# Hybrid decoder block in float32: turning the attention and retention tiles by VectorE and DRAM, and a new order on SyncE's queue

## The chip, the core and the metric

The kernel runs on one core of one Trainium2 chip. The metric is the device time of one execution in microseconds (us). PE is the matrix engine TensorE, DVE is VectorE, ACT is ScalarE, POOL is GpSimd, and SP is SyncE, which here only issues DMA transfers.

## What is computed

One decoder block over 256 tokens of width 2048, all in float32, cut here to its skeleton:

```
h = x
h = h + 0.5 * swiglu(rms_norm(h, ffn1_norm), ffn1_w_gate, ffn1_w_up, ffn1_w_down)      # width 5632
n = rms_norm(h, mix_norm)
rq, rk, rv, rg, sq, sk, sv = split(n @ w_in)          # 4 x 1024, 1024, 128, 128 columns
ret = retention(rope(rq), rope(rk), rv)               # 8 heads of 128, chunks of 128 tokens
ret = silu(rg) * group_norm(ret) * ret_gn_gain
swa = sliding_window_attention(rope(sq), rope(sk), sv, sinks)   # 16 heads of 64, 2 kv heads, window 128
h = h + concat(ret, swa) @ w_out
h = h + memory_cross_attention(rms_norm(h, xa_norm), rms_norm(mem, mem_norm), wq, wkv, wo)   # 4 heads of 512, 256 memory tokens
h = h + 0.5 * swiglu(rms_norm(h, ffn2_norm), ffn2_w_gate, ffn2_w_up, ffn2_w_down)
out = rms_norm(h, final_norm)
```

## The kernel before

**Three products for one.** Float32 precision is made from a format that PE multiplies quickly (float32r): every operand is held as a high part and a rest. A product is three matmuls (`three`, lines 456 to 458): high by high, rest by high, high by rest. Activations stand as `blk` tiles (128 x 4 blocks x 2 parts x 256 tokens).

**Steps.** The weights stream through the core once. SP loads 1 MB at a time into `wf` (128 x 2 x 1024, 3 buffers), which serves two steps. For each step ACT copies the piece into `wh` (line 70) and DVE makes `wl = wf - wh` (line 75), 4 buffers of each. A step is 12 matmuls of 512 columns into an `acc` tile, and the whole program is 772 steps: FFN1 up to step 264, then the mixer's projections (window keys, values and the first window queries to 276, the other window queries to 284, retention's queries and keys to 300, its values and gate to 316 for four heads, the same for the other four to 348), `w_out` to 380, the cross attention's keys to 412, values to 444, queries to 476, output projection to 508, FFN2 from there to the end. In `run_stream`, `prepare` issues loads and splits so that the split of a step stands three steps ahead of its use (`LOOKAHEAD = 3`).

**The order of everything else.** A clock counts steps. `later(delay, fn)` puts a task on a list, and `run_due` emits the due tasks between two steps. What a task emits for PE, ACT and DVE is pinned behind the last instruction emitted for that engine; the splits are not pinned and are placed by the scheduler. On SP and POOL the DMAs stand in the order in which the scheduler comes to them.

**Turning.** Results come with the tokens on the partitions and are wanted with the features there. `cross` does this for most tiles: DVE turns 32 x 32 blocks of a 128 x 512 tile (STREAM_TRANSPOSE, line 437), POOL's queue writes the tile to a DRAM `box` (line 439) and reads it back in four DMAs in another order (line 444), and the consumer runs `TURN = 6` steps after. Four kinds of tiles are turned on PE instead, against an identity matrix: the window attention's probabilities (`swa_group.second`, line 632), its queries, as high and rest parts (`turned` in `sq_done`, line 682), retention's output (`turn`, line 327) and the cross attention's probabilities (`attend.probs`, line 882).

**Norms.** `Norm.stat` squares (ACT) and adds (DVE) into `sums`; `Norm.finish` sums over partitions with matmuls against ones (line 397), two steps after the last block; `spread` turns the row of scales (line 413).

**Memory tokens.** While `w_out` runs, `mem_block` loads the 256 memory tokens in eight pieces into `t2k` tiles (line 805, on SP), from which nmem's blocks are made (line 349).

Of the kernel before, what the change touches and what calls it, by code (L numbers as in the profile page):

```python
# [17 lines left out]
P = 128  # L18
S = 256
# [10 lines left out]
LOOKAHEAD = 3  # L30
TAIL = 4
WARM = 9
FIRST = 16
TURN = 6
# [4 lines left out]
def decoder_block(ctx: ExitStack, tc: tile.TileContext, a: dict, out: bass.AP):  # L39
# [40 lines left out]
    identr = const.tile([P, P], F32R, tag="identr", name="identr")  # L80
# [8 lines left out]
    nc.vector.tensor_copy(identr, ident)  # L89
# [141 lines left out]
    def run_stream():  # L231
# [22 lines left out]

        def prepare(upto):
            while nxt[0] < min(upto, len(steps)):
                at = nxt[0]
                if at == len(loaded):
                    u, piece = steps[at][0], steps[at][3]
                    if u.pair:  # L260
                        loaded.extend(load_pair(u.w, piece))
                        continue
                    two = at + 1 < len(steps) and steps[at + 1][0] is u and steps[at + 1][3] == piece + 1
                    loaded.extend(load(u.w, piece, 1 + two))
# [16 lines left out]
        for at, (u, b, ks, _, first, last) in enumerate(steps):  # L281
# [4 lines left out]
            else:  # L286
# [3 lines left out]
                prepare(at + 1 + LOOKAHEAD)  # L290
            run_until(lambda: b in u.lhs)
# [30 lines left out]
    def turn(src):  # L322

        tp = [tmp_ps() for _ in range(2)]
        for kk in range(4):
            for t in range(2):
                nc.tensor.transpose(
                    tp[kk // 2][:, (kk % 2) * S + t * P : (kk % 2) * S + (t + 1) * P], src(t, kk), ident
                )
        return tp  # L330

# [19 lines left out]
    class Norm:  # L351
# [4 lines left out]
        def __init__(self, gcol, name, spread=True):  # L356
            self.gcol, self.spreads = gcol, spread
# [19 lines left out]
        def stat(self, src):  # L377
# [10 lines left out]
            if self.left == 0:  # L388
                later(2, self.finish)

        def finish(self):

            tp = tmp_ps()
            for t in range(2):
                for i in range(2):
                    at = i * S + t * P
                    nc.tensor.matmul(  # L397
                        tp[:, t : t + 1], self.sums[:, at : at + P], ones[:, :1], start=i == 0, stop=i == 1
                    )
# [7 lines left out]
        def spread(self):  # L407
# [6 lines left out]
            self.rows = work.tile([P, S], F32, tag="rows", name=nm("rows"), bufs=2)  # L414
# [14 lines left out]
    def cross(src, then, room=None, delay=TURN):  # L429
# [4 lines left out]
        out, boxes = [], []  # L434
        for i, v in enumerate(src):
            sq = t2k()
            nc.vector.transpose(sq.rearrange("p (g q j) -> p q g j", g=4, q=4), squares_of(v))  # L437
            box = dram.tile([P, 512], F32, tag="box", name=nm("box"))
            nc.gpsimd.dma_start(box, sq)  # L439
            boxes.append(box.rearrange("(i r) (g n) -> g r i n", i=4, g=4))  # L440
        for i, box in enumerate(boxes):
            dst = t2k() if room is None else room[i]
            for g in range(4):
                nc.gpsimd.dma_start(dst[32 * g : 32 * g + 32, :].rearrange("p (i n) -> p i n", i=4), box[g])  # L444
            out.append(dst.rearrange("p (i q j) -> p q i j", i=4, q=4))
# [70 lines left out]
    n1 = Norm(G_FFN1, "n1", spread=False)  # L516
    for b in range(4):
# [4 lines left out]
        later(4 * b + (b < 3), lambda b=b: n1.stat([hT[b]]))  # L522
# [9 lines left out]
    nmix = Norm(G_MIX, "nmix")  # L532
# [59 lines left out]
    def swa_group(g, t, heads, q, probs):  # L592
# [473 lines left out]
```

## Time and profile before

| | before |
|---|---|
| median of 3 runs | 2206.41 us (2206.3 to 2208.78) |
| profiled execution, its own time | 2206.03 us |
| its span in the profile | 2204.2 us |
| PE busy | 2182.6 us (99%) |
| DVE busy | 1291.2 us (59%) |
| ACT busy | 1027.3 us (47%) |
| POOL busy | 309.6 us (14%) |

PE is busy nearly all of the span. A stretch of the profile is read by asking how long PE stands idle in it, what it then waits for, and what the engine that it waits for had in front. The stages lie at these times: FFN1 to 729 us, the mixer's projections from there to 998, `w_out` to 1094, the cross attention to 1473, FFN2 behind it.

### The profile page before, as it was taken

Reading aid. Unit: us, or ns where it says so; the run is one execution under the profiler, and the core shown is the slowest. Engines: PE = TensorE matmul, PEld = TensorE weight load, DVE = VectorE, ACT = ScalarE, POOL = GpSimd, SP = SyncE. Lnnn points to the kernel's source line nnn. Section 1 sums busy time; section 2 is a strip of 40 time slices with the busy share of each in tenths; the row PEclk is TensorE's granted clock in tenths of the full one; section 3 lists DMA queues with packets and bytes.
Section 4 is the critical chain, followed back from the end, with each engine's and each line's share of the span. In section 5 each row is a group of like instructions: output and inputs, shape, how many; then the busy total and the mean of one; then the engine's idle time right before and its main releaser. Section 6 shows DMA issues by size and latency. Waiting matters only on the chain.

```text
span 2204.2 us, 25835 instructions
## 1 busy us (share of the span) xinstructions
PE 2182.6 (99%) x9868; PEld 1807.8 (82%) x9868; DVE 1291.2 (59%) x1535; ACT 1027.3 (47%) x1260; POOL 309.6 (14%) x557
## 2 busy tenths in 40 slices
PE   9999999999999999999999999999999999999998
PEld 7888888888888888888788888887888888888886
DVE  5555555555556779786655555565555544555554
ACT  6444444444445554544545554454544433444443
POOL 0200111011011110111231011123201000000100
PEclk9999999999999999999999999999999999999999
DMA  7766677666677555556776555577766655666663
GB/s 268 230 218 211 210 230 234 216 212 233 210 234 245 208 193 172 179 185 196 234 252 230 196 191 191 190 247 232 260 217 224 215 191 193 214 208 223 213 217 143
DMA packets 132731, 472.04 MB, mean 214 GB/s; under 512 B 15616, under 2 KB 16384, under 8 KB 132480
## 3 DMA queue, kind: packets, MB, share of 16 engines
q1 hardware_dynamic: 109856, 413.57, 54.8%
q0 software_dynamic: 22464, 56.66, 8.8%
q8 instruction: 77, 1.26, 0.2%
q14 instruction: 46, 0.38, 0.1%
q10 hardware_dynamic: 288, 0.18, 0.0%
HBM read 439.93 MB, written 30.41 MB: 213 GB/s over the span
## 4 chain that ended last, share of the span: by engine, by line
PE 88%; issue 5%; DMA 3%; DVE 2%; ACT 1%; POOL 1%; SPq 0%; ACTq 0%; POOLq 0%; DVEq 0%
PE acc L457 28%; PE acc L456 28%; PE acc L458 28%; DMA wf<-in_w_out 1%; DVE wl L75 1%; DMA t2k<-box 1%; DMA wf<-in_ffn_w_up 1%; ACT wh L70 1%; POOL t2k L444 1%; PE tmp L458 0%; PE tmp L457 0%; PE tmp L456 0%; PE tmp L397 0%; PE tmp L632 0%; PE tmp L606 0%
## 5 line engine op out<-in xcount | busy, mean ns | idle before, releaser
L75 DVE TENSOR_TENSOR wl<-wf,wh 128x1024 fp32r<-128x1024 f32 (+1 forms) x776 | 941.2, 1217 | 793.0 <-ACT wh L70 789.7
L70 ACT ACTIVATE wh<-wf 128x1024 fp32r<-128x1024 f32 (+1 forms) x776 | 815.8, 1055 | 977.0 <-PE acc L458 916.8
L456 PE MATMUL acc<-wh,blk 128*128 128x512 f32 (+1 forms) x3104 | 1209.7, 390 | 4.4 <-ACT wh L70 3.5
L457 PE MATMUL acc<-wl,blk 128*128 128x512 f32 (+1 forms) x3104 | 1207.2, 389 | 2.5 <-DVE wl L75 2.5
L458 PE MATMUL acc<-wh,blk 128*128 128x512 f32 (+1 forms) x3104 | 1206.4, 389 | 0.0
L456 PEld LDWEIGHTS acc<-wh,blk 128*128 128x128 f32 x3104 | 583.9, 188 | 125.5 <-ACT wh L70 4.9
L457 PEld LDWEIGHTS acc<-wl,blk 128*128 128x128 f32 x3104 | 583.9, 188 | 123.0 <-DVE wl L75 4.7
L458 PEld LDWEIGHTS acc<-wh,blk 128*128 128x128 f32 x3104 | 583.8, 188 | 120.2 <-DVE blk L349 0.2
L439 POOL DMA_DIRECT2D box<-t2k x108 | 60.8, 563 | 1516.1 <-DVE t2k L437 1483.2
L444 POOL DMA_DIRECT2D t2k<-box x432 | 236.0, 554 | 122.6 <-issue 47.0
L70 ACT ACTIVATE blk<-t2k 128x512 fp32r<-128x512 f32 (+2 forms) x74 | 45.1, 614 | 59.8 <-DMA t2k<-box 58.1
L437 DVE STREAM_TRANSPOSE t2k<-t2k 128x512 f32<-128x512 f32 x76 | 49.4, 687 | 19.0 <-ACT t2k L70 19.0
L75 DVE TENSOR_TENSOR blk<-t2k,blk 128x512 fp32r<-128x512 f32 (+1 forms) x66 | 43.7, 674 | 26.1 <-ACT blk L70 26.0
L493 ACT ACTIVATE t2k<-acc,n 128x512 f32<-128x512 f32 x44 | 27.8, 685 | 29.4 <-PE acc L458 29.4
L500 DVE SCALAR_TENSOR_TENSOR t2k<-acc,n,t2k 128x512 f32<-128x512 f32 x44 | 31.0, 746 | 7.7 <-PE acc L458 7.7
L70 ACT ACTIVATE blk<-h,gains 128x256 fp32r<-128x256 f32 x64 | 27.4, 496 | 8.7 <-DVE h L467 8.7
L70 ACT ACTIVATE blk<-tmp 128x512 fp32r<-128x512 f32 (+2 forms) x49 | 21.7, 450 | 20.2 <-DVE blk L75 14.4
L349 DVE SCALAR_TENSOR_TENSOR blk<-h,gains,blk 128x256 fp32r<-128x256 f32 x64 | 26.8, 478 | 0.0
L467 DVE TENSOR_TENSOR h<-h,t2k 128x512 f32<-128x512 f32 x32 | 21.1, 687 | 9.0 <-DMA t2k<-box 8.7
L386 DVE TENSOR_TENSOR t2k<-t2k,t2k 128x512 f32<-128x512 f32 x35 | 24.1, 687 | 1.9 <-ACT t2k L382 0.6
L75 DVE TENSOR_TENSOR blk<-tmp,blk 64x256 fp32r<-64x256 f32 (+2 forms) x41 | 19.2, 474 | 3.0 <-ACT blk L70 2.8
L382 ACT ACTIVATE t2k<-h 128x512 f32<-128x512 f32 x32 | 18.2, 616 | 2.6 <-DVE h L467 2.6
(125 smaller groups left out, 495.2 us busy)
## 6 DMA issues: line engine op xcount, KB each, us to landing
wf<-in_ffn_w_down SPq DMA_DIRECT2D x88, 1024.0 KB, 4.9
wf<-in_ffn_w_gate SPq DMA_DIRECT2D x87, 1024.0 KB, 5.1
wf<-in_ffn_w_up SPq DMA_DIRECT2D x87, 1024.0 KB, 5.6
box<-t2k POOLq DMA_DIRECT2D x108, 256.0 KB, 2.9
t2k<-box POOLq DMA_DIRECT2D x432, 64.0 KB, 4.9
wf<-in_w_in_rqk SPq DMA_DIRECT2D x16, 1024.0 KB, 5.0
wf<-in_w_in_rvg SPq DMA_DIRECT2D x16, 1024.0 KB, 5.0
wf<-in_w_out SPq DMA_DIRECT2D x16, 1024.0 KB, 5.3
```

Source lines behind the costliest of these rows:

```text
L70: return nc.scalar.activation(dst, src, AF.Copy, **kw)
L75: nc.vector.tensor_tensor(lo, src, hi, ALU.subtract)
L349: nc.vector.scalar_tensor_tensor(x[:, k, 1, :], v[:, k, :], g, x[:, k, 0, :], ALU.mult, ALU.subtract)
L386: nc.vector.tensor_tensor(self.sums, self.sums, y, ALU.add)
L437: nc.vector.transpose(sq.rearrange("p (g q j) -> p q g j", g=4, q=4), squares_of(v))
L439: nc.gpsimd.dma_start(box, sq)
L444: nc.gpsimd.dma_start(dst[32 * g : 32 * g + 32, :].rearrange("p (i n) -> p i n", i=4), box[g])
L456: nc.tensor.matmul(o, ah, bh, start=start, stop=False)
L457: nc.tensor.matmul(o, ah, bl, start=False, stop=False)
L458: nc.tensor.matmul(o, al, bh, start=False, stop=stop)
L493: nc.scalar.activation(gated[b][t], acc[:, t, :], AF.Silu, scale=norm.scale(t))
L500: nc.vector.scalar_tensor_tensor(s[t], acc[:, t, :], norm.scale(t), s[t], ALU.mult, ALU.mult)
```

## The change

1. **Queues.** `cross` becomes three tasks: DVE turns at once, `write` puts the box on SP's queue one step later, `read` puts the four reads there two steps later, and the consumer runs after `TURN = 5`. POOL issues no DMA any more; SP issues 1076 rather than 420.
2. **Loads written ahead.** `fetch` issues a load four steps (`AHEAD = 4`) before its split is prepared, so that loads stand 8 steps ahead of their use in the program.
3. **Turning.** Window probabilities, window queries, retention's output and the cross attention's probabilities go through `cross`; `turn` and `identr` are gone. Window queries are split into halves after the turning rather than before. STREAM_TRANSPOSE of tiles in SBUF goes from 76 to 100. PE loses 84 float32 transposes and 32 of the queries' kind.
4. **Norms.** `finish` first adds the two halves of `sums` on DVE and needs two matmuls rather than four; its delay is given for each norm (2, 3 or 4 steps). Only nmix spreads its scales.
5. **Smaller moves.** The memory tokens are loaded into `blk` tiles, four DMAs rather than eight; the blocks of `w_out` run 0, 2, 3, 1; nxa's blocks are made during the keys; retention's scores start a step later; `swa_values` runs four steps after the probabilities.
6. **Queries ahead of values.** The cross attention projects keys, queries, values, where it was keys, values, queries. `attend` makes scores and softmax when a query block is there, and `values` multiplies when the value block is there.

The core of the diff:

```diff
+AHEAD = 4
-TURN = 6
+TURN = 5
...
             prepare(at + 1 + LOOKAHEAD)
+            fetch(at + 1 + LOOKAHEAD + AHEAD)
...
         def finish(self):
+            x = self.sums
+            nc.vector.tensor_tensor(x[:, :S], x[:, :S], x[:, S:], ALU.add)
             tp = tmp_ps()
             for t in range(2):
-                for i in range(2):
...
+                nc.tensor.matmul(tp[:, t : t + 1], x[:, t * P : (t + 1) * P], ones[:, :1], start=True, stop=True)
...
+        sq = [t2k() for _ in src]
+        for x, v in zip(sq, src):
+            nc.vector.transpose(x.rearrange("p (g q j) -> p q g j", g=4, q=4), squares_of(v))
+        def write():
+            for x in sq:
+                boxes.append(dram.tile([P, 512], F32, tag="box", name=nm("box")))
+                nc.sync.dma_start(boxes[-1], x)
+        def read():
+            for box, dst in zip(boxes, room):
...
+                for g in range(4):
+                    nc.sync.dma_start(dst[32 * g : 32 * g + 32, :].rearrange("p (i n) -> p i n", i=4), far[g])
...
+        later(1, write)
+        later(2, read)
         later(delay, lambda: then(out))
...
-        def second():
-            tp = tmp_ps()
-            for n in range(4):
-                nc.tensor.transpose(tp[:, n * P : (n + 1) * P], s[:, n * P : (n + 1) * P], ident)
+        def second(out):
...
-        later(5, second)
+        cross([s], second, [s])
...
-            later(5, lambda: turned(0))
-            later(6, lambda: turned(1))
+            cross(rs, turned, rs)
...
-                tp = turn(lambda t, kk: ret[t][:, kk * P : (kk + 1) * P])
-                mixT[g] = split_turned(tp, G_GN + 4 * g)
-            later(3, turned)
...
+            cross(ret, turned)
...
-            nc.sync.dma_start(m[i], a["mem"][b * P : (b + 1) * P, 2 * i : 2 * i + 2, :])
+        m = st["mem"][:, 4 * (b % 2) : 4 * (b % 2) + 4, :]
+        nc.sync.dma_start(m, a["mem"][b * P : (b + 1) * P])
...
-    for i in range(4):
-        Unit(a["xa_wv"], i, 512, nmem.blocks, v_done(i), range(4))
...
     for i in range(4):
         Unit(a["xa_wq"], i, 512, nxa.blocks, put_done(nxa, queries, i, lambda i=i: attend(i)), range(4), pair=True)
+    for i in range(4):
+        Unit(a["xa_wv"], i, 512, nmem.blocks, v_done(i), range(4))
```

**How it stands on the engines: DVE at the window attention beside retention (step 326).** In the rows, `wl` names are splits, `tmp` and `m`, `den`, `es` belong to the softmax of one window group. Before:

```order
L75 TENSOR_TENSOR wl_1155_6832<-wf_1153_6829,wh_1154_6831 128x1024
L616 TENSOR_REDUCE m_1146_6806<-t2k_1143_6797 128x2
L75 TENSOR_TENSOR wl_1157_6848<-wf_1153_6829,wh_1156_6847 128x1024
L617 TENSOR_TENSOR m_1146_6806<-m_1146_6806,sinks_83 128x2
L618 TENSOR_SCALAR nmx_1147_6807<-m_1146_6806 128x2
L619 TENSOR_TENSOR es_1149_6809<-sinks_83,m_1146_6806 128x2
L75 TENSOR_TENSOR wl_1163_6885<-wf_1161_6882,wh_1162_6884 128x1024
L623 TENSOR_TENSOR den_1148_6808<-den_1148_6808,es_1149_6809 128x2
```

After, the end of a stretch of 19 rows (26 instructions) that begins with the masks of the group and has no weight split in it:

```order
L625 TENSOR_TENSOR den_1188_6991<-den_1188_6991,es_1189_6992 128x2
L626 RECIPROCAL den_1188_6991<-den_1188_6991 128x2
L627 TENSOR_TENSOR t2k_1183_6980<-t2k_1183_6980,den_1188_6991 128x512
L786 SCALAR_TENSOR_TENSOR blk_1178_6934<-t2k_1169_6873,gains_79,blk_1178_6934 128x128 x4
L76 TENSOR_TENSOR blk_901_5562<-tmp_1179_6951,blk_901_5562 64x2x128
L432 STREAM_TRANSPOSE t2k_1190_7003<-t2k_1183_6980 128x4x4x32
L76 TENSOR_TENSOR blk_901_5562<-tmp_1179_6951,blk_901_5562 64x2x128
L432 STREAM_TRANSPOSE t2k_1198_7046<-acc_1152_6804 128x4x4x32
L432 STREAM_TRANSPOSE t2k_1199_7047<-acc_1152_6804 128x4x4x32
L76 TENSOR_TENSOR blk_1191_7005<-t2k_1153_6817,blk_1191_7005 128x256 x2
L76 TENSOR_TENSOR wl_1196_7029<-wf_1175_6904,wh_1195_7028 128x1024
```

The splits that stood between the parts of one softmax now stand behind all of it, with a turning of the probabilities and two of an `acc` tile ahead of them.

**DVE in FFN2 at step 540, where the second block of columns ends.** The L500 (after: L502) rows multiply gate by up from `acc_2052` (after: `acc_2054`), whose last matmul is that of step 540. Before:

```order
L75 TENSOR_TENSOR wl_2065_12009<-wf_2063_12006,wh_2064_12008 128x1024
L75 TENSOR_TENSOR wl_2067_12027<-wf_2063_12006,wh_2066_12026 128x1024
L75 TENSOR_TENSOR wl_2070_12045<-wf_2068_12042,wh_2069_12044 128x1024
L500 SCALAR_TENSOR_TENSOR t2k_2042_11897<-acc_2052_11923,n2_109,t2k_2042_11897 128x512
L500 SCALAR_TENSOR_TENSOR t2k_2043_11898<-acc_2052_11923,n2_109,t2k_2043_11898 128x512
L437 STREAM_TRANSPOSE t2k_2071_12062<-t2k_2042_11897 128x4x4x32
L437 STREAM_TRANSPOSE t2k_2073_12066<-t2k_2043_11898 128x4x4x32
```

After:

```order
L76 TENSOR_TENSOR wl_2066_12034<-wf_2047_11928,wh_2065_12033 128x1024
L502 SCALAR_TENSOR_TENSOR t2k_2048_11942<-acc_2054_11956,n2_107,t2k_2048_11942 128x512
L502 SCALAR_TENSOR_TENSOR t2k_2049_11943<-acc_2054_11956,n2_107,t2k_2049_11943 128x512
L432 STREAM_TRANSPOSE t2k_2075_12103<-t2k_2048_11942 128x4x4x32
L432 STREAM_TRANSPOSE t2k_2076_12104<-t2k_2049_11943 128x4x4x32
L76 TENSOR_TENSOR wl_2068_12050<-wf_2059_11983,wh_2067_12049 128x1024
L76 TENSOR_TENSOR wl_2071_12068<-wf_2059_11983,wh_2070_12067 128x1024
```

Before, the splits of the next three steps stand ahead of the group that waits for the end of step 540; after, the split of the very next step, `wl_2068`, stands behind it.

**SP while `w_out` runs.** `in_w_out` rows are weight loads, `in_mem` rows the memory tokens. Before:

```order
L202 DMA wf_1361_7950<-in_w_out 128x2x1024
L202 DMA wf_1366_7984<-in_w_out 128x2x1024
L805 DMA t2k_1373_8025<-in_mem 128x512
L805 DMA t2k_1374_8026<-in_mem 128x512
L202 DMA wf_1375_8029<-in_w_out 128x2x1024
L202 DMA wf_1387_8082<-in_w_out 128x2x1024
L805 DMA t2k_1395_8130<-in_mem 128x512
```

After:

```order
L437 DMA box_1344_7788<-t2k_1339_7767 128x512
L437 DMA box_1345_7790<-t2k_1340_7768 128x512
L201 DMA wf_1348_7796<-in_w_out 128x2x1024
L444 DMA t2k_1349_7810<-box_1344_7788 32x4x128 x4
L444 DMA t2k_1350_7815<-box_1345_7790 32x4x128 x4
L201 DMA wf_1355_7840<-in_w_out 128x2x1024
L201 DMA wf_1361_7891<-in_w_out 128x2x1024
```

A box's writes and reads now stand between weight loads; each read waits for its box to have landed, and the loads behind it are issued after that.

## Rows read from the trace of the kernel before

**Rows 1.** The page: engines, and the chain that ended last, by engine.
```profile
PE 2182.6 (99%) x9868; PEld 1807.8 (82%) x9868; DVE 1291.2 (59%) x1535; ACT 1027.3 (47%) x1260; POOL 309.6 (14%) x557
...
PE 88%; issue 5%; DMA 3%; DVE 2%; ACT 1%; POOL 1%; SPq 0%; ACTq 0%; POOLq 0%; DVEq 0%
```

**Rows 2.** Timeline of PE in FFN1: start us, us, engine, line, operation; 12 matmuls apart.
```profile
399.69 0.39 PE L456 MATMUL acc<-wh,blk 128*128 128x512 f32 x1
...
402.41 0.39 PE L456 MATMUL acc<-wh,blk 128*128 128x512 f32 x1
```

**Rows 3.** Chain of waits, its PE pieces with transposes and sums: start us, us, what.
```profile
47.73 0.79 PE tmp L397 x8
...
778.25 0.64 PE tmp L682 x8
...
796.97 0.44 PE tmp L632 x4
...
1006.79 0.87 PE tmp L327 x8
...
1126.45 0.42 PE tmp L413 x2
...
1316.73 0.44 PE tmp L882 x4
```

**Rows 4.** Windows: stretch, length, busy of PE PEld DVE ACT POOL, clock, DMA share, GB/s.
```profile
764.00:998.00 234.00, 232.39 (x1139) 192.18 (x1138) 192.19 (x376) 123.47 (x215) 27.02 (x44) 1.00 0.52 178
836.00:900.00 64.00, 62.95 (x315) 51.74 (x314) 55.73 (x121) 31.94 (x56) 8.43 (x12) 1.00 0.48 163
1047.00:1092.00 45.00, 39.94 (x166) 31.81 (x165) 28.59 (x41) 23.89 (x39) 9.56 (x18) 0.96 0.78 247
1088.60:1091.50 2.90, 2.90 (x8) 2.29 (x7) 2.33 (x4) 2.90 (x7) 0.00 (x0) 0.50 0.74 250
1300.00:1312.00 12.00, 10.66 (x57) 8.91 (x56) 6.07 (x7) 4.22 (x5) 2.15 (x4) 1.00 0.76 243
...
1490.00:1502.00 12.00, 10.37 (x43) 8.27 (x42) 7.13 (x11) 5.09 (x10) 1.62 (x1) 0.86 0.54 200
```

**Rows 5.** Chain of waits while `w_out` runs.
```profile
1047.41 11.60 DMA wf<-in_w_out
...
1074.42 10.33 DMA wf<-in_w_out
```

**Rows 6.** Waits of SP's queue: us in total, times, longest.
```profile
SPq L202 <- DVE wl L75: 1399.5, 274, 11.0
...
SPq L805 <- DVE blk L349: 14.7, 2, 14.3
```

**Rows 7.** Chain of waits ahead of the first attention and of FFN2's norm.
```profile
1301.60 6.91 DMA t2k<-box
...
1484.36 6.77 DMA t2k<-box
```

**Rows 8.** The page's groups: count, busy us, mean ns, idle before and releaser.
```profile
L437 DVE STREAM_TRANSPOSE t2k<-t2k 128x512 f32<-128x512 f32 x76 | 49.4, 687 | 19.0 <-ACT t2k L70 19.0
...
L500 DVE SCALAR_TENSOR_TENSOR t2k<-acc,n,t2k 128x512 f32<-128x512 f32 x44 | 31.0, 746 | 7.7 <-PE acc L458 7.7
```

**Rows 9.** DVE's groups from 764 to 998 us, shapes apart.
```profile
L75 DVE TENSOR_TENSOR wl<-wf,wh 128x1024 fp32r<-128x1024 f32 x72 | 87.4, 1219 | 21.2 <-ACT wh L70 21.1
L611 DVE SCALAR_TENSOR_TENSOR t2k<-tmp,ctab 128x256 f32<-128x256 f32 x24 | 9.0, 415 | 1.9 <-PE tmp L606 1.9
...
L623 DVE TENSOR_TENSOR den<-den,es 128x2 f32<-128x2 f32 x8 | 1.3, 158 | 4.9 <-ACT es L622 4.9
```

**Rows 10.** The page's DMA issues: count, KB each, us from issue to landing.
```profile
box<-t2k POOLq DMA_DIRECT2D x108, 256.0 KB, 2.9
t2k<-box POOLq DMA_DIRECT2D x432, 64.0 KB, 4.9
...
wf<-in_w_out SPq DMA_DIRECT2D x16, 1024.0 KB, 5.3
```

More of the change, by code (lines that the diff above doesn't have):

```diff
@@ L253, in run_stream, with fetch @@
         nxt = [0]
+        def fetch(upto):
+            while len(loaded) < min(upto, len(steps)):
+                at = len(loaded)
+                u, piece = steps[at][0], steps[at][3]
+                if u.pair:
+                    loaded.extend(load_pair(u.w, piece))
+                else:
+                    two = at + 1 < len(steps) and steps[at + 1][0] is u and steps[at + 1][3] == piece + 1
+                    loaded.extend(load(u.w, piece, 1 + two))
         def prepare(upto):
+            fetch(upto)
             while nxt[0] < min(upto, len(steps)):
                 at = nxt[0]
[L258 to L264, printed above, removed]
                 if at == 0:
@@ L319, in run_stream @@
         pin([mybir.EngineType.SP])
[L322 to L330, printed above, removed]
     def split_turned(tp, gcol):
@@ L388, in stat @@
             if self.left == 0:
-                later(2, self.finish)
+                later(self.delay, self.finish)
         def finish(self):
+            x = self.sums
+            nc.vector.tensor_tensor(x[:, :S], x[:, :S], x[:, S:], ALU.add)
             tp = tmp_ps()
             for t in range(2):
-                for i in range(2):
[L396 to L399, printed above, removed]
+                nc.tensor.matmul(tp[:, t : t + 1], x[:, t * P : (t + 1) * P], ones[:, :1], start=True, stop=True)
             ms = sm(2, "ms")
@@ L429, in cross @@
     def cross(src, then, room=None, delay=TURN):
[L434 to L445, printed above, removed]
+        room = [None, None] if room is None else room
+        boxes = []
+        out = []
+        sq = [t2k() for _ in src]
[7 more added lines that the diff above has]
+            for box, dst in zip(boxes, room):
+                dst = t2k() if dst is None else dst
+                far = box.rearrange("(i r) (g n) -> g r i n", i=4, g=4)
+                for g in range(4):
+                    nc.sync.dma_start(dst[32 * g : 32 * g + 32, :].rearrange("p (i n) -> p i n", i=4), far[g])
+                out.append(dst.rearrange("p (i q j) -> p q i j", i=4, q=4))
+        later(1, write)
+        later(2, read)
         later(delay, lambda: then(out))
@@ L816, in out_done, with k_done, done @@
                 later(1 + 4 * b, lambda b=b: mem_block(b))
-    to_h(a["w_out"], mixT, 1.0, (2, 3, 0, 1), None, out_done)
+    to_h(a["w_out"], mixT, 1.0, (0, 2, 3, 1), None, out_done)
+    units[-4].then = units[-3]
+    def k_done(i):
+        put = put_done(nmem, keys, i)
+        def done(acc):
+            put(acc)
+            if i == 0:
+                for b in range(4):
+                    later(2 + 3 * b, lambda b=b: nxa.block(b, [hT[b]]))
+        return done
     def put_done(norm, dst, i, then=None):
@@ L900, in attend, with probs, values @@
-        later(2, probs)
+        def probs(out):
+            if i % 2 == 0:
+                st["probs"] = blk().rearrange("p k c s -> p k (c s)")
+            probs_of[i] = [st["probs"][:, 2 * (i % 2) + c, :] for c in range(2)]
+            for t in range(2):
+                hi, lo = (x.rearrange("p (m t a j) -> p t m a j", m=2, t=2, a=4)[:, t] for x in probs_of[i])
+                halves(hi, lo, out[0][:, 2 * t : 2 * t + 2])
+        cross([p], probs, [p])
+    def values(i):
+        v = vals[i]
+        ph, pl = probs_of[i]
+        o = [tmp_ps() for _ in range(2)]
+        for d in range(4):
+            ds = slice(d * P, (d + 1) * P)
+            for mt in range(2):
+                ms = slice(mt * S, (mt + 1) * S)
+                three(
+                    o[d // 2][:, (d % 2) * S : (d % 2) * S + S], v[:, 0, mt, ds], v[:, 1, mt, ds],
+                    ph[:, ms], pl[:, ms], mt == 0, mt == 1,
+                )
+        xo[i] = split_turned(o, None)
```

108 lines of the change are left out of this document (46 added, 62 removed).

## The prediction

> **What bounds the kernel now.** The page comes first: PE is busy 99% of the span and 88% of the chain that ended last is PE's own work [rows 1]. DVE, at 59%, is behind it on average. So an edit pays in three ways only: PE work that is taken out, stalls of PE that are taken out, and stalls that are put in. Second comes the timeline, for the unit of account: 12 matmuls start within 402.41 - 399.69 = 2.72 us [rows 2], so a step is 2.72 us and a matmul 0.2267 us. Third come the windows [rows 4]: the reader is to compare the length of a stretch with PE's busy time in it, and look at the clock. Three places stand out. While `w_out` runs, 45.00 - 39.94 = 5.06 us are idle, and behind the last stall the granted clock is 0.50 for 2.90 us, the lower of the two levels (1.2 rather than 2.4 GHz), which costs half of it, 1.45 us. Ahead of the first attention 12.00 - 10.66 = 1.34 us are idle. Ahead of FFN2 1.63 us are idle and the clock averages 0.86 over 12 us, another 1.7 us. Fourth come the mixer's projections, 764 to 998 us: there PE misses only 234.00 - 232.39 = 1.6 us, but DVE is busy 192.19 of 234 us (82%), and 55.73 of 64 us (87%) in its densest part, where PE already misses 1.05 us [rows 4]. That is the stage that has little room.
>
> **Part 3 of the change, turning without PE: what it takes out.** By the chain's pieces [rows 3]: 48 transposes of window probabilities at 0.44/4 = 0.11 us are 5.3; 32 of the queries at 0.64/8 = 0.08 are 2.6; 16 of retention's output at 0.87/8 = 0.109 are 1.7; 16 of the cross attention at 0.11 are 1.8. The norms (part 4) lose 20 of L397's records at 0.79/8 = 0.10, 2.0 us, and 4 of L413's at 0.21, 0.8 us. The sum is 14.2 us. All of it lies on PE, which is the path, so it is **-14**; if the first piece of each group overlaps the matmul ahead of it, some 2 us less.
>
> **What it puts on DVE.** 24 more block transposes of 0.687 us [rows 8], 20 of them between 764 and 998 us (12 for probabilities, 4 for window queries, 4 for retention): 13.7 us. Finer pieces of halves and gained tiles add, I estimate from the shapes, 3 us more. DVE's work in that stage becomes 192.2 + 17 = 209 us, while PE's becomes 232.4 less the 9.6 us of the first three terms, about 223: 94%, where it was 82%. From below: if DVE's order were perfect, it would still fit, and only stalls like today's would stay (some 3 us, since existing stalls gather). From above: if DVE could not be fuller than the 87% of the densest part, the stage would last 209/0.87 = 240 us, 17 more than PE needs.
>
> Between these ends I go by the order on DVE. Before, weight splits stand between the parts of a window group's softmax; after, at step 326, a stretch of 19 rows has none. Its two pairs of masks at 0.415 [rows 9], the reduction, eight gain pieces, the division and three transposes at 0.69 come to about 10 us, and DVE waits in the middle for ACT's exponentials (the wait for `es` sums to 4.9 us over 8 groups [rows 9], 0.6 each, more where nothing can be put in front of it): 11 to 11.5 us in all. PE meanwhile has 7 matmuls and two steps, 31 x 0.2267 = 7.0 us, until it wants `wl_1196`. That is a stall of about 4.4 us and, if the clock falls behind it as it did at 1088 us, 1.4 more. A similar heap stands at step 334 (about 2 us), and the four loads behind boxes at steps 322 to 335 are written only 4 to 7 steps ahead of use rather than 8, worth another 2 to 3; places around 290 to 316 give 2. I take **+12**, nearer to the upper end because these heaps are in the code and not a matter of chance.
>
> The Trainium skill bears on this: "VectorE: DVE Perf Modes", in its rules for kernel authors, says to use TensorE for a 128 x 128 transpose whose result may go to PSUM, and that DVE transposes only within 32 x 32 blocks. By that rule this part would be a loss where DVE is the fuller engine; by [rows 3] and [rows 8] one turning of a 128 x 512 tile is 0.44 us of PE or 0.69 us of DVE and a trip through DRAM, so the rule and the rows agree on the price and the question is only which engine ends last.
>
> **Part 1, the queues.** POOL was on no path but the reads' [rows 7], so its relief is worth nothing by itself. On SP a double turning now stands as two writes, a wait until the boxes have landed (2.9 us [rows 10]) and eight reads; with an issue of some 0.4 us each, the loads behind are held for 2 x 0.4 + 2.9 + 8 x 0.4 = 7 us. What hides that: SP waits 1399.5 us in 274 waits, 5.1 us each, for a free buffer [rows 6], a load lands in 5.3 us [rows 10], and between the freeing of a buffer and the use of its next content there are 6 steps, 16.3 us, to the split. 16.3 - 5.3 = 11 us of room against 7, with three steps (8 us) of lookahead behind. In the FFNs, with one such turning in 16 steps, I cost it at **nothing**; if two fall together, the splits' lookahead is eaten too, and beyond that each microsecond is PE's.
>
> **Step 540.** DVE after has the two products at 0.746 and their two turnings at 0.687 [rows 8] ahead of `wl_2068`, which PE wants for the step that begins when the products may. 2 x 0.746 + 2 x 0.687 + 1.22 [rows 9] = 4.1 us less a matmul and small overlaps: 3.9 us, and 1.4 for the clock: **+5.5**. Before, the splits of three steps stood ahead. This is one place; the other ends of FFN groups keep their order.
>
> **Stalls that go.** While `w_out` runs, the chain passes through weight loads of 11.60 and 10.33 us [rows 5], twice the 5.3 that such a load takes otherwise, since SP stood 14.3 us for a `t2k` buffer that nmem's blocks (L349) had not freed [rows 6], with weight loads behind. After, the tokens go into `blk` tiles, free in time, and the loads stand 8 steps ahead: 5.06 + 1.45 = **-6.5**. The first attention waited for its reads (6.91 us [rows 7]); it now runs a step later and behind fewer transfers: **-1.3**. FFN2's norm waited for the last block's reads (6.77 us [rows 7]); its finish now has 4 steps rather than 2, 5.4 us more than the 1.63 missing: 1.63 + 1.7 = **-3.3**. Each stall hides about 0.16 us more, as a matmul's record of 0.39 us outlasts its spacing of 0.2267 [rows 2]; with the mixer's old ones (1.6 us, whose heaps are replaced, not added to) I take **-3.5** for these two. The sum of the old stalls is -14.6. What is late next: nmem's finish, with its power on POOL, and the first `attend`, each under a microsecond: **+1.5** for all small places.
>
> **Sum**, against the profiled execution's own 2206.0 us (the median of the runs is 2206.4, so nothing is to be corrected): 2206.0 - 14.2 - 14.6 + 12 + 5.5 + 1.5 = **2196 us**.
>
> **The rivals.**
>
> *Clean.* DVE's heaps cost little because a step's splits stand 3 ahead and the engine catches up between: +4 in the mixer's stage, step 540 without the clock's fall +4: 2206.0 - 28.8 + 4 + 4 + 1 = 2186. For it: 209 us of work does fit into 223. Against: 87% fullness already cost 1.05 us in 64 [rows 4].
>
> *DVE becomes the bound in the mixer's stage.* At 87% at most, the stage costs +17, with the loads written late +20: 2196 + 8 = 2204, and 2210 where the clock falls at every stall. For it: the split-free stretch; against: DVE's small pieces are no harder to fill than splits.
>
> *SP's queue becomes the bound; slower.* About 40 double turnings hold the loads 7 us each. If eight reads were issued at the rate of a landing rather than an issue, or if the reads wait behind 1 MB loads in the transfer engines, the box's landing goes from 2.9 to 8 us or more, the hold from 7 to 12, past the 11 us of room; it decides from there, and each further microsecond counts some 40 times where lookahead doesn't recover: with half a microsecond lost at each, +20: 2216. For it: reads of 64 KB already take 4.9 us [rows 10] at shares of 0.5 to 0.78 of the transfer engines [rows 4]. Against: SP's 5.1 us of slack per load.
>
> The Trainium skill names the rule behind this: "DMA: Bandwidth & Descriptors", under the heading that issuing engines are not separate DMA queues, says that the engine which issues must wait on the first transfer's semaphore before it issues one that depends on it. The trace does not show SP do so for a box; SP's wait for a buffer [rows 6] shows what stands behind such a wait.
>
> *No effect.* The transposes' time was covered by DVE's lag, so taking them out gives nothing: 2206.0 - 11 (stalls) + 12 = 2207. For it: nothing but the dense stage; against: chain pieces of PE directly behind one another [rows 3].
>
> **How the numbers follow.** Forecast (2190 to 2202) 0.50; clean (2178 to 2190) 0.16; DVE the bound (2202 to 2211) 0.17; no effect 0.05; SP the bound or other mishaps of its kind (over 2211) 0.12. A measurement of this kernel tells 0.2%, 4.4 us, from no change. Faster than 2202: 0.66; within: 0.22; slower than 2210.8: 0.12. The range from 2183 to 2211 leaves out SP's case and the better part of the clean one, about 0.18.
>
> **What would show it.** Right: no idle PE and clock 1.00 while `w_out` runs; PE some 84 + 32 transposes shorter, 2170 us busy; a stall of about 4 us with a release by `wl` where FFN2's second block of columns ends; PE idle some 10 us in the mixer's stage with DVE over 90% and `wl` as releaser. Wrong: `wf` as the end of PE's or ACT's waits in many places (SP the bound), or a mixer's stage shorter than 224 us (clean).

## The result, and the profile after

The changed kernel is slower: 2217.98 us (2212.78 to 2218.68, 5 runs) against 2206.41 us (2206.03 to 2211.41), a ratio of 1.0044 (1.0028 to 1.0059). The forecast was 2196 us, in 2183 to 2211. The profiled execution of after took 2212.78 us, the shortest of its five, with a span of 2211.0 us; so the trace explains +6.8 us of span, and some 5 us of the medians' difference lie in executions of which no trace was kept.

The engines of after, from the page; the row of before is in [rows 1]:

```profile
PE 2173.6 (98%) x9732; PEld 1796.6 (81%) x9732; DVE 1308.3 (59%) x1575; ACT 1023.7 (46%) x1266; POOL 12.6 (1%) x17
```

PE does 9 us less work in a span that is 6.8 us longer. The stages say where. Each number is the time from the end of PE's last `acc` matmul before the first step named to the end of the last one before the second, read from the trace (the first row from the span's start, the last row to the last of these matmuls):

| steps | before | after | difference |
|---|---|---|---|
| 0 to 276 | 764.2 | 762.4 | -1.8 |
| 276 to 348, the mixer | 234.5 | 246.7 | +12.2 |
| 348 to 380, `w_out` | 95.7 | 88.5 | -7.2 |
| 380 to 508, cross attention | 378.3 | 373.6 | -4.7 |
| 508 to 524 | 47.9 | 44.3 | -3.6 |
| 524 to 540 | 43.5 | 50.4 | +6.9 |
| 540 to 556 | 44.0 | 49.0 | +5.0 |
| 556 to the end | 587.6 | 587.6 | 0.0 |

The windows of after (columns as in [rows 4]) show the same places:

```profile
762.00:1009.00 247.00, 229.87 (x1055) 187.10 (x1053) 202.22 (x393) 120.02 (x214) 3.93 (x3) 0.99 0.63 207
808.00:837.00 29.00, 25.73 (x110) 20.56 (x110) 23.59 (x41) 15.31 (x30) 0.00 (x0) 0.94 0.79 245
837.00:866.00 29.00, 26.46 (x119) 21.79 (x118) 26.01 (x43) 11.32 (x21) 0.00 (x0) 0.94 0.70 227
948.70:976.00 27.30, 24.16 (x107) 19.06 (x105) 20.35 (x35) 10.29 (x22) 0.00 (x0) 1.00 0.57 181
1053.90:1097.50 43.60, 43.60 (x194) 36.08 (x194) 31.07 (x39) 23.67 (x32) 0.00 (x0) 1.00 0.86 289
1490.00:1500.00 10.00, 10.00 (x47) 8.04 (x46) 7.51 (x12) 6.43 (x10) 0.70 (x1) 1.00 0.54 188
1540.00:1572.00 32.00, 23.76 (x93) 18.53 (x92) 14.36 (x16) 13.71 (x16) 0.00 (x0) 0.92 0.65 218
```

Compare length and PE's busy time. The mixer has 17 us idle where it had 1.6. `w_out` and the start of FFN2's norm, which had 5.06 and 1.63 us idle [rows 4], now have none. FFN2 from 1540 to 1572 us, full before, has 8.2 us idle. DVE in the mixer is busy 202 of 247 us, 82% as before; its share did not change, its order did.

What PE waits for in after (total us, times, longest), over the whole span:

```profile
PE acc L459 <- DVE wl L76: 16.9, 14, 3.5
PE acc L458 <- ACT wh L71: 6.3, 3, 3.9
```

Both are the split of a weight piece that comes too late. SP's waits in after:

```profile
SPq L201 <- DVE wl L76: 828.9, 224, 8.7
SPq L437 <- DVE t2k L432: 345.6, 103, 13.7
...
SPq L444 <- DMA box<-t2k: 76.8, 34, 8.0
```

The second row is a wait that the prediction didn't have: a box write (L437) stands at the head of SP's queue until DVE has turned its tile, and weight loads stand behind it. In the mixer alone (762 to 1009 us) this wait, and ACT's waits for loads that land late, are in after:

```profile
SPq L437 <- DVE t2k L432: 95.1, 17, 13.4
```

```profile
ACT wh L71 <- DMA wf<-in_w_in_rvg: 18.6, 7, 5.6
...
ACT wh L71 <- DMA wf<-in_w_in_rqk: 13.7, 7, 4.4
```

Before, ACT waits for no load from 764 to 998 us. Waits for `wf` are what the prediction named as the sign of SP's queue being the bound.

**The mixer.** DVE in after near step 326, the place of the second order fence (start us, us; idle before in brackets):

```profile
919.02 0.74 DVE L613 SCALAR_TENSOR_TENSOR t2k<-tmp,ctab 128x256 f32<-128x256 f32 x2
...
923.73 0.16 DVE L625 TENSOR_TENSOR den<-den,es 128x2 f32<-128x2 f32 x1 [1.20 <-ACT es L624]
...
926.12 0.69 DVE L432 STREAM_TRANSPOSE t2k<-t2k 128x512 f32<-128x512 f32 x1
...
927.29 1.31 DVE L432 STREAM_TRANSPOSE t2k<-acc 128x512 f32<-128x512 f32 x2
...
929.31 2.35 DVE L76 TENSOR_TENSOR wl<-wf,wh 128x1024 fp32r<-128x1024 f32 x2
```

For 10.3 us, from 919.02 to 929.31, no split runs; PE loses 3.1 us in two stalls at its end (2.04 and 1.04). More is lost earlier: steps 292 to 308 take 58.1 us where they took 51.1. PE stands 2.79 us at 815.8 and 2.54 us at 843.3, both times for `wl`, and the granted clock averages 0.94 in the two windows around them. DVE in after ahead of the second stall:

```profile
833.33 1.22 DVE L76 TENSOR_TENSOR wl<-wf,wh 128x1024 fp32r<-128x1024 f32 x1
...
838.49 0.71 DVE L432 STREAM_TRANSPOSE t2k<-t2k 128x512 f32<-128x512 f32 x1
...
844.61 1.22 DVE L76 TENSOR_TENSOR wl<-wf,wh 128x1024 fp32r<-128x1024 f32 x1
```

Some 10 us without a split again: a softmax, the turning of its probabilities and seven pieces of the rotation (rope) of retention's tiles. SP near step 334 in after:

```profile
958.83 10.16 SPq L437 DMA_DIRECT2D box<-t2k  x3
969.09 0.38 SPq L195 DMA_DIRECT2D wf<-in_w_in_rvg  x1
969.57 7.47 SPq L444 DMA_DIRECT2D t2k<-box  x12
977.08 0.94 SPq L195 DMA_DIRECT2D wf<-in_w_in_rvg  x2
```

Three box writes take 10.16 us, since the third waits for DVE, and twelve reads 7.47: in 18 us SP issues one load.

**FFN2.** The step 540, DVE in after:

```profile
1565.94 1.41 DVE L502 SCALAR_TENSOR_TENSOR t2k<-acc,n,t2k 128x512 f32<-128x512 f32 x2 [7.70 <-PE acc L460]
1567.26 1.29 DVE L432 STREAM_TRANSPOSE t2k<-t2k 128x512 f32<-128x512 f32 x2
1568.48 4.59 DVE L76 TENSOR_TENSOR wl<-wf,wh 128x1024 fp32r<-128x1024 f32 x4
```

This is the stall that was forecast: DVE waits 7.70 us for the end of the step, then does products and turnings, then the split that PE wants. Four steps earlier, at step 536, PE waits for a load; the chain of after (start us, us, what):

```profile
1534.21 6.36 DMA box<-t2k
...
1545.15 5.73 DMA wf<-in_ffn_w_up
```

SP issued a box write at 1534.21, right behind a 1 MB load; the write landed after 6.36 us, 0.65 us behind that load, rather than after the 2.1 us that are the median after the change (page, DMA issues). Its reads could not be issued before 1540.59, and the next load stood behind them until 1545.15. PE's row there is

```profile
1552.10 0.49 PE L458 MATMUL acc<-wh,blk 128*128 128x512 f32 x1 [3.93 <-ACT wh L71]
```

### The profile page after: what moved, and what is told of

It is laid out like the page before. It is cut to its first block, busy times and chain, and to the rows that moved or that the text cites. A ratio compares the mean times of both kernels' runs of the same rounds, so it can differ in the third digit from the quotient of the medians.

```text
span 2211.0 us, 25687 instructions
## 1 busy us (share of the span) xinstructions
PE 2173.6 (98%) x9732; PEld 1796.6 (81%) x9732; DVE 1308.3 (59%) x1575; ACT 1023.7 (46%) x1266; POOL 12.6 (1%) x17
## 4 chain that ended last, share of the span: by engine, by line
PE 51%; DVE 2%; DMA 2%; issue 1%; SPq 0%; ACT 0%; POOL 0%; ACTq 0%; POOLq 0%; DVEq 0%
PE acc L459 17%; PE acc L460 17%; PE acc L458 17%; DMA box<-t2k 1%; DVE wl L76 1%; DMA wf<-in_w_in_rvg 0%; DMA t2k<-box 0%; PE tmp L460 0%; PE tmp L459 0%; PE tmp L458 0%; SPq L444 0%; DVE t2k L432 0%; DMA wf<-in_ffn_w_up 0%; ACT wh L71 0%; POOL gnr L758 0%
## 5 line engine op out<-in xcount | busy, mean ns | idle before, releaser
L459 PE MATMUL acc<-wl,blk 128*128 128x512 f32 (+1 forms) x3104 | 1209.5, 390 | 17.0 <-DVE wl L76 16.9
L458 PE MATMUL acc<-wh,blk 128*128 128x512 f32 (+1 forms) x3104 | 1208.7, 389 | 6.3 <-ACT wh L71 6.3
L458 PEld LDWEIGHTS acc<-wh,blk 128*128 128x128 f32 x3104 | 584.5, 188 | 128.1 <-ACT wh L71 8.1
L432 DVE STREAM_TRANSPOSE t2k<-t2k 128x512 f32<-128x512 f32 x100 | 65.9, 691 | 16.6 <-ACT t2k L71 16.4
L71 ACT ACTIVATE blk<-t2k 128x512 fp32r<-128x512 f32 (+4 forms) x102 | 55.5, 561 | 14.8 <-DMA t2k<-box 14.5
L76 DVE TENSOR_TENSOR blk<-t2k,blk 128x512 fp32r<-128x512 f32 (+3 forms) x94 | 55.6, 607 | 2.4 <-ACT blk L71 1.9
L502 DVE SCALAR_TENSOR_TENSOR t2k<-acc,n,t2k 128x512 f32<-128x512 f32 x44 | 31.0, 747 | 15.3 <-PE acc L460 15.3
L623 ACT ACTIVATE t2k<-t2k,nmx 128x128 f32<-128x128 f32 (+1 forms) x32 | 14.3, 446 | 40.6 <-DVE nmx L620 40.6
L459 PE MATMUL tmp<-blk,blk 128*128 128x256 f32 (+1 forms) x80 | 23.1, 289 | 0.8 <-DVE blk L76 0.8
L460 PE MATMUL tmp<-blk,blk 128*128 128x256 f32 (+1 forms) x80 | 23.2, 290 | 0.0
L71 ACT ACTIVATE blk<-tmp 64x256 fp32r<-64x256 f32 (+1 forms) x25 | 11.2, 455 | 25.7 <-PE tmp L460 17.9
L458 PE MATMUL tmp<-blk,blk 128*128 128x256 f32 (+1 forms) x80 | 22.9, 286 | 0.0
```

The costliest lines, as they stand in the source:

```text
L71: return nc.scalar.activation(dst, src, AF.Copy, **kw)
L76: nc.vector.tensor_tensor(lo, src, hi, ALU.subtract)
L432: nc.vector.transpose(x.rearrange("p (g q j) -> p q g j", g=4, q=4), squares_of(v))
L458: nc.tensor.matmul(o, ah, bh, start=start, stop=False)
L459: nc.tensor.matmul(o, ah, bl, start=False, stop=False)
L460: nc.tensor.matmul(o, al, bh, start=False, stop=stop)
```

## The experiments

Two theories for the mixer. **D**: the added turnings on DVE push splits back. **Q** (later **L**): boxes on SP hold the weight loads. Each ratio below sets a run against executions of before taken beside it.

**pool.** Boxes on POOL's queue again:

```diff
-                nc.sync.dma_start(boxes[-1], x)
+                nc.gpsimd.dma_start(boxes[-1], x)
-                    nc.sync.dma_start(dst[32 * g : 32 * g + 32, :]...
+                    nc.gpsimd.dma_start(dst[32 * g : 32 * g + 32, :]...
```

> The changed kernel with the box writes and reads on POOL's queue as before; tasks, delays, turnings and loads written ahead stay. Theory Q (the boxes on SP hold the weight loads, in fact and in the order in which the splits were put on DVE): the mixer's stage (steps 276 to 348) falls from 246.7 us to 226 to 232, the stretch of steps 524 to 556 from 99.4 to 87.5 as before the change, in all 2180 to 2190 us. Theory D (the 24 added turnings fill DVE, whatever the queue): the mixer's stage stays at 242 to 248, steps 524 to 556 fall, in all 2198 to 2206 us.

2260.53 us (1.0246 of before, 1.0229 to 1.0264): both expectations fell. The waits of PE in pool:

```profile
PE tmp L458 <- ACT blk L71: 22.0, 6, 9.9
PE tmp L392 <- DVE t2k L389: 11.4, 3, 4.8
PE acc L459 <- DVE wl L76: 5.0, 8, 1.0
```

The split's waits shrink to 5.0 us, in the mixer from 13.3 us (`wl` and `wh`) to 0.5, and ACT waits there for no load: with every turning still on DVE, the splits are in time once the boxes have left SP's queue. PE's other stalls, 23 us idle in the mixer, gave the splits time too, so 0.5 is not a clean share. PE now waits for consumers of the turned tiles: attention scores (L458 into `tmp`) and the norms' sums (L392). From the trace's issue and landing times of each box write and its four reads, the trip from DVE's turning to the last read's landing takes 12.9 us in the median here and 9.2 in after; 48 of 132 trips take longer than the 5 steps (13.6 us) that `TURN = 5` gives. Steps 524 to 556 fall to 94.7 us only, not to 87.5.

**pe_all.** The four kinds turned on PE, as before; boxes on SP. The `second` of the window group, for one:

```diff
-        cross([s], second, [s])
+            tp = tmp_ps()
+            for n in range(4):
+                nc.tensor.transpose(tp[:, n * P : (n + 1) * P], s[:, n * P : (n + 1) * P], ident)
...
+        later(5, second)
```

> The changed kernel with the four kinds of tiles turned on PE as before; boxes stay on SP's queue. Theory Q: PE gets its 9.6 us back in the mixer's stage and fewer boxes stand ahead of loads there, 236 to 242 us rather than 246.7; steps 524 to 556 stay at 98 to 100; in all 2206 to 2212 us. Theory D: the mixer's stage returns to 232 to 236; in all 2200 to 2206 us.

2201.82 us (0.9984, 0.9975 to 0.9994). The mixer's stage returns to 233.3 us, as theory D had it, though PE has its 9.6 us of transposes back. The run also takes 24 boxes off SP's queue, and ACT waits for no load in the mixer, so by itself it doesn't tell D from Q. Steps 524 to 556 stay long, 101.7 us.

**pool_pe.** Both undone.

> Both undone: boxes on POOL's queue and the four kinds turned on PE; the norms, the memory tokens, loads written ahead, queries ahead of values stay. Theory Q: some 11 us more than the run with POOL's queue alone, 2192 to 2200 us. Theory D: 8 to 14 us less than the run with POOL's queue alone, 2190 to 2196 us. Both: steps 524 to 556 at 87.5, w_out (steps 348 to 380) near 88 us rather than the 95.8 of before.

2214.05 us (1.0043, 1.0028 to 1.0058), slower than both theories: steps 380 to 412 take 98.9 us and 508 to 524 49.3, where pe_all has 88.7 and 44.2. PE waits there for the norms' sums, 8.8 us in two waits. Steps 524 to 556 take 98.1 us, where both theories had 87.5.

**h_pool.** Only the four turnings of h, at the start of FFN2, on POOL's queue.

```diff
-        cross([hT[b]... for t in range(2)], made)
+        cross([hT[b]... for t in range(2)], made, queue=nc.gpsimd)
```

> The changed kernel with only the four turnings of h at the start of FFN2 on POOL's queue. Both theories: everything to step 508 as in the changed kernel; steps 524 to 556 fall from 99.4 us to 87.5 if boxes on SP made both stalls there (the load that PE waits for at 1548 us and the split behind the products at 1566 us): 12 us less, 2200 to 2206 us. If the split stands behind the products for another reason, only the first 5 us go.

2210.76 us (1.0027, 1.0017 to 1.0037). Steps 540 to 556 fall to 43.5, so the split's place at step 540 was made by these boxes. Steps 524 to 540 stay at 51.1 us: there, ACT's copy of the turned h (into `blk`) waits for late reads over POOL, with a split (`wh`) behind it on ACT, as the chain of h_pool shows. The box write was as slow from POOL's queue:

```profile
1532.24 6.88 DMA box<-t2k
...
1543.32 6.98 DMA t2k<-box
...
1550.41 0.09 ACT blk L71
...
1550.94 1.05 ACT wh L71
```

**spread_h.** Boxes on SP, the turnings of h 16 steps apart:

```diff
-                later(6 + 4 * b, lambda b=b: turn_h(b))
+                later(19 + 16 * b, lambda b=b: turn_h(b))
```

> The changed kernel with the four turnings of h put 16 steps apart, from step 532 on and between the FFN's own turnings, rather than 4 steps apart from step 519 on; all boxes on SP. If it is the crowd of boxes on SP that makes both stalls at the start of FFN2 (a box issued behind a 1 MB load lands after 6 to 7 us, its reads hold the next load; and the split of step 540 is put behind the products), steps 524 to 556 fall from 99.4 us to 87 to 88, in all 2201 to 2206 us. If queries ahead of values or the loads written ahead make them, they stay at 95 to 100.

2201.13 us (0.9978, 0.9966 to 0.9990). Steps 524 to 556 take 87.0 us; the window of both, after first, shows it:

```profile
1515.00:1572.00 57.00, 48.76 (x203) 39.24 (x202) 28.65 (x32) 23.85 (x29) 0.00 (x0) 0.96 0.74 239
```

```profile
1515.00:1572.00 57.00, 57.00 (x253) 47.20 (x252) 33.75 (x35) 26.04 (x28) 0.00 (x0) 1.00 0.73 244
```

The crowd of four turnings in 12 steps made both stalls of FFN2.

**pe_spread.** pe_all and spread_h together.

> The four kinds of tiles turned on PE (as in the run pe_all) and h's turnings 16 steps apart. If the two losses are separate, they add: the mixer's stage at 233 us as in pe_all, steps 524 to 556 at 87.5 rather than 101.7, in all 2201.8 - 14 = 2186 to 2190 us, less than either kernel. If PE only waits elsewhere, 2195 or more.

2187.97 us (0.9919, 0.9900 to 0.9938): the two losses are separate and add. PE's waits for `wl` fall from 16.9 us in after to 0.4.

**noturn and noload.** Each leaves out a part of the mixer's load: noturn the block transposes, noload three quarters of the bytes of retention's weight loads. Neither takes a box off SP's queue; noload makes the loads behind the boxes shorter, not free:

```diff
+        sq = src if plain else [t2k() for _ in src]
+            if plain:
+                continue
             nc.vector.transpose(...)
...
-        nc.sync.dma_start(wf, w[:, piece].rearrange("f p n -> p f n"))
+        nc.sync.dma_start(wf[:, :, :few], w[:, piece].rearrange("f p n -> p f n")[:, :, :few])
```

> The changed kernel without the 20 block transposes on DVE of window probabilities, window queries and retention's output (the tile goes to its box as it is): the computation is changed there, all transfers, tasks and the order of tasks stay. Theory D (DVE's added work, 13.7 us, makes the mixer's stalls): steps 276 to 348 fall from 246.7 us to 228 to 236. Theory L (loads held by the boxes on SP make them): they stay at 243 to 247.

> The changed kernel with the weight loads of retention's projections (steps 284 to 348) cut to a quarter, 256 KB, the split reading that quarter four times: the result there is changed, DVE's, ACT's and PE's work and all boxes stay. Theory L: the mixer's stage falls from 246.7 us to 225 to 234. Theory D: it stays at 240 to 247, since only the stalls near 926 and 976 us have a load in them.

noturn took 2202.93 us, its mixer's stage (276 to 348) 237.0; noload 2210.38 us, the stage 241.0. Against after's 246.7 leaving out the turnings gives back 9.7 us and shortening the loads 5.7. noturn lies 1.0 us above theory D's range and noload inside it, but neither alone reaches the 233.3 of pe_all. noload is not a full test of theory L: ACT still waits 28.8 us for loads in the stage, where after has 32.3. In noturn these waits fall to 20.9 us, though no load was changed: less work on DVE makes the loads less late.

**some_dve and swa_spread.** Which of the turnings costs. In some_dve window probabilities and retention's output are on PE, in swa_spread only the window probabilities; both have h's turnings apart.

> Window queries and the cross attention's probabilities turned by DVE and DRAM as in the changed kernel, window probabilities and retention's output on PE; h's turnings 16 steps apart. Theory D with its place (what costs is DVE's work between steps 292 and 348, while the turned queries at 276 to 292 and the cross attention have room on DVE): steps 276 to 292 at 45.8 us as in the changed kernel, 292 to 348 at 183 to 185, 412 to 476 at 195; in all some 5 us less than pe_spread's 2188.0, 2182 to 2185 us. If any turning taken from PE comes back as a stall, 2187 to 2192.

> The changed kernel with only the window probabilities back on PE, and h's turnings 16 steps apart. Theory D: 12 of the 20 added turnings leave DVE, 8.2 us, and 5.3 us of PE come back; steps 292 to 348 fall from 201 us to 186 to 190; in all 2184 to 2190 us. If retention's own turnings and gain pieces make the stalls, they stay at 195 to 201.

some_dve: 2186.57 us (0.9916, 0.9898 to 0.9933). swa_spread: 2184.33 us (0.9907, 0.9886 to 0.9928), the lowest ratio here, though its interval overlaps those of some_dve and pe_spread. In swa_spread steps 292 to 348 take 184.3 us, where spread_h, which differs in the probabilities alone, takes 201.9. That is 17.6 us; steps 276 to 292 are 2.4 us shorter in spread_h (45.8 against 48.2), so moving the probabilities costs the mixer's stage 15.3 us. The other eight turnings just pay: steps 276 to 348 take 232.4 us in swa_spread and 233.3 in pe_spread, 0.9 us less for 4.3 us of PE work saved. The gain expected of some_dve was 5 us; by the traces it is 2.7: steps 276 to 292 take 47.9 us rather than the 45.8 expected, and 412 to 476 195.6.

**pool_turn6.** pool_pe with one step more for the trip, and nmem's norm finished after 3 steps rather than 4:

```diff
-TURN = 5
+TURN = 6
...
-    nmem = Norm(G_MEM, "nmem", 4)
+    nmem = Norm(G_MEM, "nmem", 3)
```

> The run pool_pe (boxes on POOL's queue, four kinds turned on PE) with TURN = 6 rather than 5, and nmem's finish after 3 steps rather than 4. If the box's trip over POOL (12.7 us in the middle, 26 of 108 over 5 steps) is what made pool_pe 12 us slower than pe_all, the waits of the norms' finishes go: steps 380 to 412 from 98.9 to 88 to 90 us, 508 to 524 from 49.3 to 44 to 47; in all 2198 to 2204 us. If something else of POOL's queue makes it, 2210 to 2216.

2188.71 us (0.9927, 0.9899 to 0.9954), below what was expected. Steps 380 to 412 take 88.4 us, 508 to 524 44.1, and 524 to 556 88.7 with h's turnings in their old crowd. Boxes on POOL with six steps are as good as boxes on SP with five and h spread (pe_spread).

**pe_ahead0.** Boxes on SP, but loads only 4 steps ahead:

```diff
-AHEAD = 4
+AHEAD = 0
```

> pe_spread (2188.0 us) with AHEAD = 0: loads are written 4 steps ahead of use as before, boxes stay on SP. If loads must stand ahead of the boxes' waits on SP's queue, each box now holds the load of a near step: 2195 to 2215 us, with waits of wh for wf near the turnings. If the splits' lookahead covers it, 2186 to 2190.

2257.33 us (1.0237, 1.0218 to 1.0255), 69 us more than pe_spread and beyond what was expected. FFN1 alone, steps 16 to 264, goes from 674.8 to 690.4 us. ACT's waits in pe_ahead0:

```profile
ACT wh L71 <- DMA wf<-in_ffn_w_gate: 234.0, 43, 9.1
ACT wh L71 <- DMA wf<-in_ffn_w_down: 103.9, 29, 7.4
```

Splits wait for loads all through the program. With boxes on SP, loads have to stand ahead.

**noboth and noturn_swa.** What was left open by noturn and noload:

> The cuts of noturn (20 block transposes left out) and of noload (retention's weight loads a quarter) together; the results there are changed. If DVE's turnings and the held loads are the two causes of the mixer's stalls, nothing else is left: steps 276 to 348 at 223 to 228 us, near what PE's work alone needs. If the longer way of the probabilities (write, read, split as tasks of their own, several steps later) puts heaps on DVE by itself, 231 to 237, as in noturn alone (237.0).

> The changed kernel without the 12 block transposes of the window probabilities alone (the result there is changed). If these 12 carry the cost of DVE's added work, steps 276 to 348 fall from 246.8 us to 237 to 240, as in noturn; if the eight of queries and retention's output carry their share by count, 241 to 244.

noboth: 2195.00 us, the mixer's stage 226.7, inside the 223 to 228 expected if nothing else is left. What it shows is that less work on DVE and shorter loads together remove the stalls; the boxes still stand on SP's queue there, and ACT waits 13.8 us for loads. noturn_swa: 2208.80 us, the stage 240.6, between the two expectations; 6.1 of noturn's 9.7 us belong to the probabilities. Windows of the mixer, after, noboth and swa_spread:

```profile
764.00:1000.00 236.00, 218.87 (x1000) 177.86 (x1000) 194.77 (x367) 111.82 (x206) 2.92 (x2) 0.99 0.62 201
```

```profile
764.00:1000.00 236.00, 232.51 (x1095) 192.44 (x1094) 200.80 (x390) 126.05 (x220) 5.84 (x4) 1.00 0.38 120
```

```profile
764.00:1000.00 236.00, 232.61 (x1117) 192.35 (x1116) 203.18 (x394) 123.30 (x218) 4.03 (x4) 1.00 0.58 194
```

In the same 236 us DVE does more work in swa_spread (203.18 us, 86%) than in after (194.77 us, 83%), and PE is idle 3.4 us rather than 17.1.

## Why the prediction was wrong

**Right, by size.** The step-540 stall: +5.5 forecast, steps 540 to 556 +5.0; that the crowd of h's boxes makes it (spread_h, h_pool) was not foreseen. `w_out`: -6.5 forecast, -7.2; without the loads written ahead it takes 94.8 us (pe_ahead0), so the memory tokens' new tiles alone did not bring it. The norm ahead of FFN2: -3.3 forecast, 508 to 524 -3.6. PE's busy time was forecast at 2170 us and is 2173.6. The heap near step 326 was forecast as a stall of 4.4 us with 11 to 11.5 us of DVE; it has 10.3 us of DVE and 3.1 of stall.

**Mis-sized: the mixer's new stalls, +12.** The stage grew by 12.2 us although PE lost 9.6 us of work there, so 22 us of stalls came in; the forecast's terms for this stage (-9.6 for PE, -1.6 of old stalls, +12) give about +1. The size was too small by some 11 us, and even the rival of a DVE bound at 87% (240 us for the stage) was too mild. By place, the term that failed is "places around 290 to 316 give 2": in steps 292 to 308 PE is idle 5.8 us, and the clock, at 0.94 over twice 29 us, takes another 3.5 by estimate (0.06 x 58), 9.3 in all. Steps 330 to 338 have 3.1 us of stall against 2, and steps 338 to 348 have 3.0 against the 2 to 3 given to late loads. Only the heap at step 326 had been priced instruction by instruction.

Its reasoning failed too. DVE was to be over 90% full with 209 us of work; it had 202 and was 82% full. swa_spread runs with 3.4 us idle at 86%, and after stalls at 83%. What counts is the order on DVE and its tie to SP: a turning late on DVE holds the box write on SP (95.1 us of waits in the mixer), that holds weight loads (ACT waits 32.3 us for them), and late loads make splits late. Without the boxes on SP (pool) PE's waits for splits in the stage are 0.5 us, and without the window probabilities' turnings and their boxes (swa_spread) 0.4, against 13.3. I priced heaps and late loads as separate places and added them. noturn (9.7) and noload (5.7) give back 15.4 us one by one and noboth 20.0 together. That the whole is more than the sum would fit a loop, but also two waits that end nearly together; which of them it is was not shown.

**Wrong: the queues at nothing.** The other step that failed is "I cost it at nothing" in part 1, where the hold of a double turning was put at 7 us against 11 of room. The prediction named the case in which two fall together, but counted one turning in 16 steps and passed over the four of h, which stand 4 steps apart in the code. The mechanism of the SP rival was right, its number of places not: the box's landing goes from 2.1 to 6.36 us behind a 1 MB load, and four turnings follow each other in 12 steps at the start of FFN2. One load came late there, and steps 524 to 540 lost 6.9 us; elsewhere in the FFNs, with one turning in 16 steps, nothing was lost, as forecast. spread_h shows the cause by removing both FFN2 stalls. The rival's 40 places would have needed loads near their use: pe_ahead0 is that case, and it costs 69 us. Together the two steps make up the miss of the profiled execution, 2212.8 against 2196 us: some 11 us in the mixer and 6.9 here, less some 2 us that the other places came out better.

**Wrong, without effect on the sum: POOL's relief "is worth nothing by itself".** At `TURN = 5` the shorter trip over SP (9.2 us rather than 12.9) is what makes the turned tiles come in time; with its boxes on POOL the changed kernel takes 43 us more (ratios 1.0246 and 1.0044). At `TURN = 6`, and with the four kinds on PE, the forecast's sentence holds: the ratios of pool_turn6 (0.9927) and pe_spread (0.9919) lie in each other's intervals.

**The rules of the Trainium skill.** "VectorE: DVE Perf Modes" prefers TensorE for a 128 x 128 transpose. For the window probabilities this case bears it out: 48 transposes of 0.11 us on PE were replaced, and the stage became 15.3 us longer. For the other turnings it doesn't: swa_spread, with queries, retention's output and the cross attention's probabilities on DVE, is by the traces 0.9 us shorter in the mixer and 1.9 us in steps 412 to 476 than pe_spread. Little, but not a loss. The prediction's other rule, to wait on the first transfer before issuing one that depends on it, stands in "DMA: Bandwidth & Descriptors" of the Trainium skill under the heading that two DMAs through the same engine are not ordered, not under the one that the prediction names. After shows SP do so: 76.8 us of waits of the reads (L444) for their boxes.

**What stays open.** The other executions of after are 3.4 to 5.9 us longer than the profiled one. No trace tells where, but their granted clock is on record: 0.996 in the profiled execution, 0.993 or 0.994 in the four others. A mean clock lower by 0.002 to 0.003 over 2211 us is, by estimate, 4.4 to 6.6 us of PE's time, so the clock behind stalls can account for all of it. All executions of pe_spread, some_dve and swa_spread, which have next to no stalls, are at 0.999, and those of one kernel lie within 1.7 us of each other. noturn_swa says that the probabilities' transposes on DVE account for 6.1 us, while moving the probabilities as a whole costs 15.3; the rest is laid to their boxes and the late loads, but no run took out the probabilities' boxes alone. The norms and the new order of queries and values were not undone in any run, so their shares are not shown.

## What to carry to other kernels

On an engine that feeds PE, look at the longest stretch without a feeding instruction and compare it with what PE has in store; the engine's average share says little. A queue that waits for a producer passes the wait on to all that stands behind it, so before moving transfers onto the queue of the loads, count what each of them waits for, the producer's work included, and put the loads ahead and the transfers apart. Price two such delays together where one can cause the other.

## What the runs showed of the hardware

In these runs a 256 KB write landed behind the 1 MB loads that were in flight. In after, the six box writes that SP issued within 0.3 us of a load landed some 0.65 us after that load, 6.36 to 9.17 us after their issue; the 72 with no load in flight took 2.1 us in the median. It is not a matter of SP's queue: in h_pool the eight boxes that POOL wrote, each with a load in flight, took 5.9 us in the median. The whole trip, a write and four dependent reads, took 9.2 us from SP's queue and 12.9 from POOL's; the page puts the write's landing at 2.1 and 2.9 us and the reads' at 4.6 and 5.3. Not each stall lowers the granted clock. Windows of after, behind the stall of 2.79 us at 815.8 us and behind that of 2.64 us at 955.0 us:

```profile
818.50:824.00 5.50, 5.44 (x17) 4.31 (x18) 4.17 (x12) 3.46 (x9) 0.00 (x0) 0.69 1.00 342
...
957.60:962.00 4.40, 4.37 (x18) 3.37 (x19) 4.40 (x8) 1.71 (x3) 0.00 (x0) 1.00 1.00 380
```

The forecast added 1.4 us for the clock behind a long stall; behind the second nothing was due in this execution.
